# Moving one filler piece in an attention loop from step (5,4) to step (6,2), and splitting the output weights by column halves

## The chip, the cores and the metric

The kernel runs on one core of one Trainium2 chip. The metric is device time in microseconds (us) of one execution. A core has five engines that run side by side, each with its own queue: TensorE (PE in the profile, with its weight loads as PEld), VectorE (DVE), ScalarE (ACT), GpSimd (POOL) and SyncE (SP), which here only issues DMAs. Matmuls write into PSUM, which has eight banks of 128 x 512 fp32 values.

## The reference

One decoder block over 1024 tokens of width 1024, fp32. Eight attention heads of width 64 with a forget gate stand beside eight groups of a gated spatial mix; both go through one output projection; then comes a gated feed-forward part with a causal convolution of width 3.

```python
xn = rmsnorm(h, norm_mix_g);  proj = xn @ w_in
c = cumsum(log_sigmoid(proj[..., G_END:] + b_forget))
p = softmax(q k^T / 8 + c_q - c_k, causal);  att = p v
sg = u * (tril(w_s) @ rmsnorm(vg, v_gain) + b_s)        # u, vg = gelu(...)
h = h + concat(att, sg) @ w_out
h = h + (silu(conv(g)) * conv(a)) @ w_down              # a, g = rmsnorm(h) @ w_up
out = rmsnorm(h, norm_final_g)
```

The rows 512 to 1023 of `w_out` belong to `sg` and are called the gated half of the projection here; the rows 0 to 511 belong to `att`.

## The kernel before

Every fp32 operand of a matmul is split into a high part (a rounded copy, on ACT or POOL) and a low part (the difference, on DVE or POOL), and a product is three matmuls: high by high, high by low, low by high. A 128 x 1024 weight is loaded by one DMA into a tile with the tag `raw` (four buffers), and the two parts of its halves are made from there.

The attention part is a list of 40 steps (h, s): eight heads, h = 0 to 7, of five steps, s = 0 to 4. In each step TensorE's order is written out by hand (`seq` chains each matmul behind the last one). Per step:

- the transposes of the probabilities for the next step (`turn_p`, L1025): two groups of four 128 x 128 blocks, each group in a PSUM bank with the tag `b`; in s = 3 and s = 4 the groups are cut differently, but it is always one bank for a group. ACT makes the high part (L1026), then DVE the low part (L1027), and then the bank is free again;
- the products with V for this step's two groups (`values`, L1041), whose sums stand in further `b` banks until ACT (L1049) and DVE (L1050) have taken them;
- the logits of the next head (L977, L978), into two tiles of two banks; DVE adds the mask and takes the row minimum (L990), ACT takes the exponential (L1000). The last head has no next one, so its steps have no logits;
- where the table `FILLS` has the step, a filler piece.

There are four `b` banks in all: for the transposes, for the sums of the products with V, for the transposed row sums (L939), and for the filler pieces.

The filler is the gated half of the output projection, `sg_out`: 16 pieces (two column halves of eight token tiles). A piece is 12 matmuls of 512 columns (L1065 to L1067), an addition of the input rows on DVE (L1069), a store of the sum to memory (`hpd`, L1070, SP), and, ahead of them, a load of the input rows into a `raw` buffer (L1061, SP). Three pieces stand before the loop, and 13 at (0,0), (0,2), (0,4) and at (h,2) and (h,4) for h = 1 to 5; the last one at (5,4). A piece reads the gated half's weights, four tiles `whl` of 128 x 2 x 512, and the transposed gate outputs `sgT`, four tiles with the tag `G`.

These two sets of buffers are used again. The attention half's weights (`wo_load`, called in program order at (7,0)) go, for the row blocks k = 0 and 1, into the four `whl` tiles, and for k = 2 and 3 into two `G` tiles; the attention outputs of the heads 4 and 5 (`pair_half(2)`, L951 to L953, POOL) and of the heads 6 and 7 (`pair_half(3)`, L955 to L957, DVE and ACT) go into the other two `G` tiles. So all of these wait for the last filler piece. The weights' splits are on POOL: a cast (L1096) and a subtraction (L1097) for each of the two column halves of each k.

After the loop comes the attention half of the output projection, `wmm` (L1271 to L1273): for the first four token tiles the blocks k = 0, 1, 2 for the column half 0 of all four tiles, then the same for the column half 1, then k = 3 for both. DVE adds `hpd` (`hadd`, L1281), ACT and DVE normalise (L1288 to L1291), and TensorE transposes (`flip`, L1309) between the products of the later token tiles. The up projection's first weights (`upw_a`, L1220; `upw_b`, L1239) are loaded into `raw` buffers that the attention weights free; their splits are on ACT (L160) and DVE (L166), their sums on POOL (L1243 to L1251). `row_tail` sends a head's row sums through memory to a broadcast tile (ACT's DMA L941, SP's DMA L942), which `pair_half` multiplies with.

TensorE's order is by hand, while the order on DVE, ACT, POOL and SP inside the loop is set by a planner that takes, at each point of its own model of time, the earliest instruction in program order that is ready; so an instruction can stand in its queue ahead of one that comes earlier in the code. Each queue runs in order: a DMA on SP that waits holds back those behind it.

Of the kernel before, what the change touches and what calls it, by code (L numbers as in the profile page):

```python
# [12 lines left out]
ALU = mybir.AluOpType  # L13
# [6 lines left out]
WARM = 8  # L20

FILLS = {(-1, j): 1 for j in (6, 4, 2)} | {(h, s): 1 for h in range(6) for s in ((0, 2, 4) if h == 0 else (2, 4))}
FCFG = ("b", 4, 4)


# [38 lines left out]
def after(tc, later, earlier):  # L64
    tc.add_manual_dep(later.ins, earlier.ins.name, mybir.DependencyInfo(
        mybir.DependencyClass.NoSync, mybir.DependencyReason.DATA), reason="order")
# [3 lines left out]
def block_kernel(ctx: ExitStack, tc: tile.TileContext, xT, xtok, wuv, wv0, wva, wvk, wvl, wqk, cpk, bfv,  # L70
                 ggain, g2r, gfr, wsp, woa, wos, wup, wdn, out):
    nc = tc.nc
    act, dve, pool, pe, sp = Line(nc.scalar, tc), Line(nc.vector, tc), Line(nc.gpsimd, tc), nc.tensor, nc.sync
# [6 lines left out]
    drm = ctx.enter_context(tc.tile_pool(name="drm", bufs=1, space=bass.MemoryType.DRAM))  # L80
    FILL = FILLS
    FTAG, FB, BB = FCFG
    psa = tc.alloc_tile_pool(name="psa", bufs=4, space=bass.MemoryType.PSUM)
# [12 lines left out]
    def sb(tag, shape, dt=F32):  # L96
        return (raws if tag == "raw" else late if tag in LATE else early).tile(shape, dt, tag=tag, bufs=BUFS[tag], name=nm(tag))
# [10 lines left out]
    def f32(ap):  # L108
        return ap.bitcast(F32)
# [75 lines left out]
    def xs(n, hl, k):  # L185
        return XS[n][k // 2][:, hl, k % 2, :]
# [7 lines left out]
    def xr(n, k):  # L194
        return RAW[n][k // 2][:, k % 2, :]
# [8 lines left out]
    def ring(dt=F32R, n=512):  # L204
        rn[0] += 1
        return sb(RTAG[(rn[0] - 1) % 6], [P, 2, n], dt)
# [76 lines left out]
    w = ring()  # L283
    split_w(ua[0][:, 0, :], (w[:, 0], w[:, 1]), "dve")
    for o in (slice(0, 256), slice(256, 512)):
        h, l, src = xs("B11", 0, 0)[:, o], xs("B11", 1, 0)[:, o], xr("x11", 0)[:, o]
# [483 lines left out]
    def sg_load(hf, floor=None):  # L770

        wrs = []
        for kp in range(2):
            wr = sb("raw", [P, 2, 512])
            queued[:] = [sp.dma_start(out=wr, in_=wos[hf, kp])]
            after(tc, queued[0], floor or loads[0])
            wrs += [wr[:, 0, :], wr[:, 1, :]]
        return wrs
# [88 lines left out]
    def head_loads(h):  # L867
        ab = sb("x1", [P, 2, 1024], F32R)
        abs_[h] = ab
        hh = h % 2  # L870
        sp.dma_start(out=f32(ab[:, 0, :]), in_=qd[h].rearrange("s d t -> (s d) t"))
        for s in range(2):
            sp.dma_start(out=f32(ab[s * 64:s * 64 + 64, 1, :]), in_=kd[h, 0])
        sp.dma_start(out=f32(a2s[0:64, hh, :]), in_=qd[h, 0])
        if h == 1:
            sp.dma_start(out=f32(a2s[64:67, hh, :]), in_=ncd[0:3, 0, :])
        loads[h] = sp.dma_start(out=f32(b2s[0:64, hh, :]), in_=kd[h, 1])
        if h:
            loads[h] = sp.dma_start(out=f32(b2s[64:67, hh, :]), in_=ncd[1:4, 1 + h, :])
        rows[h] = sml.tile([P, 8], F32, tag="rs", name=nm("rs"))  # L880

    whs, wrs = [], sg_load(0, floors["sp"])
# [62 lines left out]
    def pair_half(p, o):  # L945

        if attT[p] is None:
            attT[p] = sb("A" if p < 2 else "G", [P, 2, 1024], F32R)
        f, t = attF[p], attT[p]
        if p < 3:  # L950
            pool.tensor_tensor(out=f[:, 0, o], in0=f[:, 0, o], in1=f[:, 1, o], op=ALU.mult)  # L951
            pool.tensor_copy(t[:, 0, o], f[:, 0, o])
            pool.tensor_tensor(out=t[:, 1, o], in0=f[:, 0, o], in1=f32(t[:, 0, o]), op=ALU.subtract)  # L953
        else:
            dve.tensor_tensor(out=f[:, 0, o], in0=f[:, 0, o], in1=f[:, 1, o], op=ALU.mult)  # L955
            act.copy(t[:, 0, o], f[:, 0, o])
            dve.tensor_tensor(out=t[:, 1, o], in0=f[:, 0, o], in1=f32(t[:, 0, o]), op=ALU.subtract)  # L957
# [5 lines left out]
    def place():  # L963
        return psa.tile([P, 1024], F32, tag="L", bufs=2, name=nm("pl"))
# [53 lines left out]
    def turn_p(g):  # L1018

        ptr = bank()  # L1020
        pt = sb("pt", [P, 2, 512], F32R)
        for half, k, j0, c, w in spans(g):
            for j in range(j0, 4 * half + 4):
                o = c + (j - j0) * P
                seq(pe.transpose(ptr[:, o:o + P], places[g[0], j // 2][j % 2][:, k * P:(k + 1) * P], ident))  # L1025
        casts.append(act.copy(pt[:, 0, :], ptr))  # L1026
        los.append(dve.tensor_tensor(out=pt[:, 1, :], in0=ptr, in1=f32(pt[:, 0, :]), op=ALU.subtract))  # L1027
        return pt
# [3 lines left out]
    def values(g, pt):  # L1032
        h, x = g[0], None
        for half, k, j, c, w in spans(g):
            new = (half, k) in ((1, 0), (0, 2))
            if new:
                po[half] = bank()
            o = (j - 4 * half) * P
            for s in range(2):
                lhs = V[k // 2][:, k % 2, h, :, :].rearrange("p s d -> p (s d)")  # L1040
                seq(pe.matmul(po[half][:, o:o + w], lhs, pt[:, s, c:c + w], start=(new and s == 0),  # L1041
                              stop=(s == 1 and (half, k) in ((1, 6), (0, 3))), skip_group_check=True))
            if (half, k) in ((1, 6), (0, 3)):
                p, hh = h // 2, h % 2
                q = slice(half * 512, half * 512 + 512)
                r = slice(hh * 64, hh * 64 + 64)
                if attF[p] is None:
                    attF[p] = sb("H", [P, 2, 1024])
                x = act.copy(attF[p][r, 0, q], po[half][64:128, :])  # L1049
                dve.tensor_tensor(out=attF[p][r, 0, q], in0=po[half][0:64, :], in1=attF[p][r, 0, q], op=ALU.add)  # L1050
        return x
# [30 lines left out]

    wo = []

    def wo_load(ks):
        for k in ks:
            wr = sb("raw", [P, 1024])
            after(tc, sp.dma_start(out=wr, in_=woa[k]), loads[6])
            if k < 2:
                w = [sb("whl", [P, 2, 512], F32R) for _ in range(2)]  # L1090
            else:
                t = sb("G", [P, 2, 1024], F32R)
                w = [t[:, :, hf * 512:hf * 512 + 512] for hf in range(2)]
            for hf in range(2):
                src = wr[:, hf * 512:hf * 512 + 512]
                pool.tensor_copy(w[hf][:, 0], src)  # L1096
                pool.tensor_tensor(out=w[hf][:, 1], in0=src, in1=f32(w[hf][:, 0]), op=ALU.subtract)  # L1097
            wo.append(w)

    STEPS = [[(h, g) for g in GROUPS[n:n + 2]] for h in range(8) for n in range(0, 9, 2)]  # L1100

# [34 lines left out]
    for n, step in enumerate(STEPS):  # L1136
        h, s = n // 5, n % 5
        if s == 0 and h < 6:
            head_loads(h + 2)
        if h == 7 and s == 0:  # L1140
            for _ in filler:
                pass
            wo_load((0, 1))
            wo_load((2, 3))
        if h in (2, 4, 6) and s == 4:
            for o in (slice(0, 512), slice(512, 1024)):
                pair_half(h // 2 - 1, o)
        now, turned = turned, [turn_p(g) for g in STEPS[n + 1]] if n + 1 < len(STEPS) else []
        last, due = due, []
        if n == 34:  # L1150

            held, last = last, []
        if n == 35:
            held, last = last, held
        if n == 36:
            last = held
        if s == 1 and h % 2 == 0:
            attF[h // 2] = sb("H", [P, 2, 1024])
        if s == (1 if h < 7 else 2):
            recips[h] = dve.reciprocal(rows[h], rows[h])  # L1160
        out_copy = None
        for c, (g, pt, js) in enumerate(zip(step, now, NEXT[s])):
            out_copy = values(g, pt) or out_copy
            last_copy = out_copy
            if h < 7:
                for j in js:
                    due.append((h + 1, j, logits_min(h + 1, j, logits_mm(h + 1, j, place()))))
            if s == (1 if h < 7 else 2) and c == (h == 7):
                row_tail(h)

        for e in last:
            x = logits_exp(*e)
            after(tc, x, out_copy or casts[-1])
        fill((h, s))
        if n == 2:
            vh = sb("A", [P, 2, 4, 256])
            sp.dma_start(out=vh, in_=vu.rearrange("h p m c -> p h m c"))
        if n in UPPER:
            tt = UPPER.index(n)
            low = evac_v(tt, 1, vh[:, tt // 4, tt % 4, :])  # L1180
            after(tc, low(), los[-1])
            after(tc, vhigh[0], exs[-1])
# [155 lines left out]
    prev = None  # L1338
    for tt in (0, 4, 1, 5, 2, 3, 6, 7):
# [12 lines left out]
        prev = tt  # L1352
# [458 lines left out]
```

## Time and profile before

| | |
|---|---|
| median of 3 runs | 1050.65 us (1050.4 to 1051.11) |
| the profiled execution | 1051.8 us, of which the span is 1050.1 us |
| TensorE busy | 1038.9 us, 99% of the span |
| VectorE, ScalarE, GpSimd busy | 891.3, 563.4, 218.8 us |
| granted clock of TensorE | 0.998 of full speed |

The span has these stretches around the change: attention with its fillers from about 214 us to 363.2 us, of which 322.0 to 340.3 is head 5, 340.4 to 353.3 head 6 and 353.3 to 363.2 head 7; the attention half of the output projection from 363.2 to 412.6; the up projection after it. Times inside the span are counted from its start. A matmul of 512 columns is shown with a duration of 0.39 us, but the next one starts 0.23 us after it, so distances between starts are read, not durations.

### The profile page before, as it was taken

The numbers are of one execution on the slowest core, as the hardware profiler recorded it, in microseconds if no ns is written. First come the engines' busy times: TensorE is split into PE (matmuls) and PEld (weight loads), VectorE is DVE, ScalarE is ACT, GpSimd is POOL, SyncE is SP. The second block draws the span as 40 slices with busy tenths as digits, with TensorE's granted clock in tenths as the row PEclk, the third lists the DMA queues.
The fourth block names the chain that finished last, engine by engine and source line by source line (L and its number), as shares of the span: only waits on it lengthen the run. The fifth ranks groups of instructions, "written<-read, shape, count | busy, mean of one in ns | idle before, by whom it ended". The sixth has DMA issues, their size and how long they took to land.

```text
span 1050.1 us, 14270 instructions
## 1 busy us (share of the span) xinstructions
PE 1038.9 (99%) x4998; PEld 870.7 (83%) x4998; DVE 891.3 (85%) x1302; ACT 563.4 (54%) x1003; POOL 218.8 (21%) x165
## 2 busy tenths in 40 slices
PE   8999999999999999999999999999999999999997
PEld 6988888988888888888888888888888888888886
DVE  6898887888887779998999989899897866897774
ACT  6777533457776746644444444444444554454654
POOL 0000241400421640344333423323331000000000
PEclk9999999999999999999999999999999999999999
DMA  9622558785655544222255332332322998333442
GB/s 335 217 96 81 160 151 250 221 257 177 192 153 161 171 153 149 80 97 84 85 179 168 122 117 74 131 120 70 128 83 81 304 346 299 104 99 98 143 120 100
DMA packets 67451, 161.66 MB, mean 154 GB/s; under 512 B 8094, under 2 KB 9238, under 8 KB 67380
## 3 DMA queue, kind: packets, MB, share of 16 engines
q1 hardware_dynamic: 67108, 160.72, 47.5%
q8 instruction: 39, 0.64, 0.3%
q14 instruction: 32, 0.26, 0.1%
q10 hardware_dynamic: 272, 0.04, 0.0%
HBM read 115.68 MB, written 45.05 MB: 153 GB/s over the span
## 4 chain that ended last, share of the span: by engine, by line
PE 91%; DVE 3%; DMA 3%; ACT 2%; issue 1%; SPq 0%; POOL 0%; ACTq 0%; POOLq 0%; DVEq 0%
PE k L1624 20%; PE qc L1364 11%; PE qa L1364 11%; PE qd L1364 11%; PE qb L1364 5%; PE pb L270 5%; PE ps L270 5%; PE pb L1041 2%; PE pb L1025 2%; PE qc L510 2%; PE qd L510 2%; PE qa L510 2%; PE pl L977 1%; PE pl L978 1%; PE pf L1065 1%; PE pf L1067 1%
## 5 line engine op out<-in xcount | busy, mean ns | idle before, releaser
L1624 PE MATMUL k<-whb,wha 128*128 128x512 f32 (+1 forms) x936 | 209.8, 386 | 0.0
L1624 PEld LDWEIGHTS k<-whb,wha 128*128 128x128 f32 x936 | 174.1, 188 | 35.8 <-DVE wha L166 0.2
L1364 PE MATMUL qc<-xT,whb 128*128 128x512 f32 x540 | 129.9, 389 | 0.2 <-ACT whb L160 0.2
L1364 PE MATMUL qa<-xB,wha 128*128 128x512 f32 x528 | 127.4, 390 | 0.0
L1364 PEld LDWEIGHTS qc<-xT,whb 128*128 128x128 f32 x540 | 101.3, 188 | 21.6 <-ACT whb L160 0.5
L1364 PEld LDWEIGHTS qa<-xB,wha 128*128 128x128 f32 x528 | 98.8, 188 | 20.8 <-DVE wha L166 0.4
L160 ACT CAST wha<-sg 128x512 fp32r<-128x512 f32 x77 | 47.7, 622 | 96.6 <-PE k L1624 83.8
L160 ACT CAST whb<-sg 128x512 fp32r<-128x512 f32 x82 | 50.6, 618 | 87.6 <-PE qc L1364 67.4
L166 DVE TENSOR_TENSOR wha<-sg,wha 128x512 fp32r<-128x512 f32 x77 | 52.7, 687 | 39.3 <-ACT wha L160 39.0
L1364 PE MATMUL qd<-xB,whb 128*128 128x512 f32 x264 | 63.7, 389 | 0.0
L1364 PE MATMUL qd<-xT,whb 128*128 128x512 f32 x264 | 63.7, 389 | 0.0
L1364 PE MATMUL qb<-xT,whb 128*128 128x512 f32 x252 | 61.0, 389 | 0.0
L1026 ACT CAST pt<-pb 128x512 fp32r<-128x512 f32 x72 | 40.4, 585 | 38.2 <-PE pb L1025 33.1
L166 DVE TENSOR_TENSOR whb<-sg,whb 128x512 fp32r<-128x512 f32 x82 | 57.0, 697 | 4.4 <-ACT whb L160 4.3
L1248 POOL TENSOR_TENSOR sg<-raw 128x512 f32<-128x512 f32 x20 | 31.2, 1562 | 140.0 <-DVE whb L166 79.9
L1364 PEld LDWEIGHTS qd<-xT,whb 128*128 128x128 f32 x264 | 49.5, 188 | 10.5 <-DVE u L1471 0.3
L1364 PEld LDWEIGHTS qd<-xB,whb 128*128 128x128 f32 x264 | 49.6, 188 | 10.3
L1027 DVE TENSOR_TENSOR pt<-pb,pt 128x512 fp32r<-128x512 f32 x72 | 47.2, 686 | 11.6 <-ACT pt L1026 11.1
L1364 PEld LDWEIGHTS qb<-xT,whb 128*128 128x128 f32 x252 | 47.2, 188 | 10.0 <-DVE whb L166 0.3
L1041 PE MATMUL pb<-pt,V 128*128 128x512 f32 (+3 forms) x192 | 49.6, 362 | 0.4 <-DVE pt L1027 0.3
L1251 POOL TENSOR_TENSOR sg<-sg,raw 128x512 f32<-128x512 f32 x20 | 33.3, 1665 | 63.5 <-DVE whb L166 63.5
L1249 POOL TENSOR_TENSOR sg<-sg,raw 128x512 f32<-128x512 f32 x20 | 35.2, 1758 | 47.2 <-issue 44.6
(422 smaller groups left out, 2243.4 us busy)
## 6 DMA issues: line engine op xcount, KB each, us to landing
raw<-wup SPq DMA_DIRECT2D x44, 512.0 KB
sg<-hx SPq DMA_DIRECT2D x77, 256.0 KB
hx<-hs SPq DMA_DIRECT2D x44, 256.0 KB
hx<-ca SPq DMA_DIRECT2D x35, 256.0 KB
xT<-wdn SPq DMA_DIRECT2D x28, 256.0 KB
x<-kd SPq DMA_DIRECT2D x24, 256.0 KB
A<-xtok SPq DMA_DIRECT2D x8, 512.0 KB
raw<-wqk SPq DMA_DIRECT2D x8, 512.0 KB
```

Source lines behind the costliest of these rows:

```text
L160: act.copy(h, src)
L166: return eng.tensor_tensor(out=l, in0=src, in1=f32(h), op=ALU.subtract)
L270: pe.matmul(banks[m], xs(n, xi, k)[:, ms], w[:, wi, :], start=(first and k == 0 and c == 0 and (own or m % 2 == 0)), stop=(k == 3 and c == ...
L510: pe.matmul(ps, w[:, wi, ks], xs(n, xi, k), start=(first and c == 0), stop=(c == 11), skip_group_check=True)
L1026: casts.append(act.copy(pt[:, 0, :], ptr))
L1027: los.append(dve.tensor_tensor(out=pt[:, 1, :], in0=ptr, in1=f32(pt[:, 0, :]), op=ALU.subtract))
L1041: seq(pe.matmul(po[half][:, o:o + w], lhs, pt[:, s, c:c + w], start=(new and s == 0), stop=(s == 1 and (half, k) in ((1, 6), (0, 3))), ski ...
L1248: pool.tensor_tensor(out=s[0], in0=a21, in1=a22, op=ALU.add)
L1249: pool.tensor_tensor(out=s[1], in0=s[0], in1=a11, op=ALU.add)
L1251: pool.tensor_tensor(out=s[3], in0=s[1], in1=a12, op=ALU.add)
L1364: pe.matmul(ps, w[:, wi, ks], xb[:, xi, k, :], start=(first and n == 0), stop=(n == 11), skip_group_check=True)
L1624: pe.matmul((banks[bk + m] if ps is None else ps)[:, o], xh[:, xi, ms], wh[:, wi, o], start=((first and p_ == 0 or new) and n == 0), stop= ...
```

## The change

Two edits. The 16th filler piece is issued at step (6,2) instead of at (5,4). And the splits of the attention weights, which went k by k (both column halves of k = 0, then of k = 1, and so on), go by column halves: half 0 of k = 0, 1, 2; half 1 of k = 0, 1, 2; then both halves of k = 3. They are chained, each cast behind the subtraction before it. The four loads come in the same order as before, now all ahead of the first split in program order.

```diff
 FILLS = {(-1, j): 1 for j in (6, 4, 2)} | {(h, s): 1 for h in range(6) for s in ((0, 2, 4) if h == 0 else (2, 4))}
+FILLS[6, 2] = FILLS.pop((5, 4))
...
-    def wo_load(ks):
-        for k in ks:
+    def wo_load():
+        wrs = []
+        for k in range(4):
             wr = sb("raw", [P, 1024])
             after(tc, sp.dma_start(out=wr, in_=woa[k]), loads[6])
             if k < 2:
...
                 t = sb("G", [P, 2, 1024], F32R)
                 w = [t[:, :, hf * 512:hf * 512 + 512] for hf in range(2)]
-            for hf in range(2):
-                src = wr[:, hf * 512:hf * 512 + 512]
-                pool.tensor_copy(w[hf][:, 0], src)
-                pool.tensor_tensor(out=w[hf][:, 1], in0=src, in1=f32(w[hf][:, 0]), op=ALU.subtract)
+            wrs.append(wr)
             wo.append(w)
+        prev = None
+        for k, hf in [(k, hf) for hf in range(2) for k in range(3)] + [(3, 0), (3, 1)]:
+            w, src = wo[k][hf], wrs[k][:, hf * 512:hf * 512 + 512]
+            c = pool.tensor_copy(w[:, 0], src)
+            if prev is not None:
+                after(tc, c, prev)
+            prev = pool.tensor_tensor(out=w[:, 1], in0=src, in1=f32(w[:, 0]), op=ALU.subtract)
...
         if h == 7 and s == 0:
             for _ in filler:
                 pass
-            wo_load((0, 1))
-            wo_load((2, 3))
+            wo_load()
```

## The prediction

> **What bounds the kernel now.** I read the busy table, the chain of waits, TensorE's waits by releaser, and then the timelines of the engines from 334 to 386 us, where the moved piece, its old and new place and everything that waits for its buffers lie.
>
> ```profile
> PE 1038.9 (99%) x4998; PEld 870.7 (83%) x4998; DVE 891.3 (85%) x1302; ACT 563.4 (54%) x1003; POOL 218.8 (21%) x165
> PE 91%; DVE 3%; DMA 3%; ACT 2%; issue 1%; SPq 0%; POOL 0%; ACTq 0%; POOLq 0%; DVEq 0%
> PE pb L1025 <- DVE pt L1027: 0.9, 1, 0.9
> 340.30:353.30 13.00, 13.00 (x86) 11.64 (x84) 11.97 (x25) 9.59 (x22) 13.00 (x15) 1.00 0.40 135
> 353.30:363.20 9.90, 8.65 (x56) 6.83 (x55) 7.56 (x16) 7.44 (x18) 4.65 (x5) 1.00 0.52 152
> 363.20:412.60 49.40, 49.39 (x243) 40.82 (x242) 38.63 (x59) 26.17 (x52) 11.26 (x8) 1.00 0.48 175
> ```
>
> TensorE sets the time. Moving a piece changes none of its work, so the change is worth only what it adds to or takes from TensorE's gaps. In the stretches around the piece the waits view names a wait of 0.9 us on DVE's low part, and the window rows (length, then busy time of PE, PEld, DVE, ACT, POOL, clock, DMA) put the open time into head 7: 9.90 - 8.65 = 1.25 us. The output projection behind it has none. The clock is 1.00 everywhere.
>
> The gap that matters stands where head 6 ends, and beside it stands the same place one head earlier, which has the piece:
>
> ```profile
> 334.34 0.27 PE L1025 MATMUL pb<-ident,gg 128*128 128x128 f32 x1
> 336.12 1.06 PE L1025 MATMUL pb<-ident,t 128*128 128x128 f32 x8
> 337.54 0.45 PE L1065 MATMUL pf<-whl,G 128*128 128x512 f32 x1
> 340.36 1.03 PE L1025 MATMUL pb<-ident,t 128*128 128x128 f32 x8
> 343.92 1.04 PE L1025 MATMUL pb<-ident,t 128*128 128x128 f32 x8
> 347.18 0.41 PE L1025 MATMUL pb<-ident,t 128*128 128x128 f32 x2
> 349.94 0.27 PE L1025 MATMUL pb<-ident,gg 128*128 128x128 f32 x1
> 351.91 1.08 PE L1025 MATMUL pb<-ident,H 128*128 128x128 f32 x8
> 353.34 0.62 PE L1025 MATMUL pb<-ident,H 128*128 128x128 f32 x4
> 354.86 0.66 PE L1025 MATMUL pb<-ident,H 128*128 128x128 f32 x4 [0.90 <-DVE pt L1027]
> 355.46 1.20 PE L1041 MATMUL pb<-pt,V 128*128 128x512 f32 x4
> ```
>
> These rows are the step starts: (5,3) at 334.34, (5,4) at 336.12, the piece at 337.54, (6,0) at 340.36, (6,1) 343.92, (6,2) 347.18, (6,3) 349.94, (6,4) 351.91, (7,0) 353.34. At (7,0) TensorE turns one group of four blocks and stops: the second group needs a `b` bank, and all four are held, two by the transposes of 351.91, one by the sums of head 6, one by the group just turned. The bank comes when the low part of the 351.91 group is done. At (6,0) the same eight transposes run without a stop, since the piece stands ahead of them. The Trainium skill (Perfetto Trace Analysis, Optimization Strategy) says that the same gap in a saturated engine, coming back, can mean too few PSUM tiles to give out. The trace agrees so far as it has one such place; by that rule a second place without a piece gets a second gap, as the sum below has it from rows.
>
> **Part one: the piece leaves (5,4).** TensorE reaches (6,0) at 337.54 instead of 340.36: 2.82 us early. The bank there comes from these:
>
> ```profile
> 336.91 0.60 ACT L1000 ACTIVATE wy<-wy,mn 128x384 f32<-128x384 f32 x1
> 337.63 1.07 ACT L1026 CAST pt<-pb 128x512 fp32r<-128x512 f32 x2
> 338.25 1.29 DVE L1027 TENSOR_TENSOR pt<-pb,pt 128x512 fp32r<-128x512 f32 x2 [0.34 <-ACT pt L1026]
> 341.94 1.29 DVE L1027 TENSOR_TENSOR pt<-pb,pt 128x512 fp32r<-128x512 f32 x2 [0.70 <-ACT pt L1026]
> 343.15 1.33 DVE L990 CUSTOM_DVE_ANT_0 H<-pl,t,lim 128x1024 f32<-128x1024 f32 x1
> 353.50 1.07 ACT L1026 CAST pt<-pb 128x512 fp32r<-128x512 f32 x2
> 354.12 1.29 DVE L1027 TENSOR_TENSOR pt<-pb,pt 128x512 fp32r<-128x512 f32 x2 [0.45 <-ACT pt L1026]
> ```
>
> The low part of the first group starts at 338.25 and takes half of 1.29 and a little, so the bank is there at about 339.0; TensorE stands from 337.94 (four transposes take 0.4) to 339.0: 1.06 us. The next bank, for the sums of head 6, comes with the second low part at 339.55, so the products start at 339.6: with 0.82 us of transposes a step starting at 337.54 wanted them at 338.36, a loss of 1.25 us. The gap at (7,0) confirms the size: there 355.46 - 353.34 - 0.82 = 1.30 us.
>
> Then (6,0) to (6,2) follow, 3.56, 3.26 and 2.76 us long by the starts above. DVE could be the next to stop TensorE: after its 0.70 us of idle time at 341.94 it works nearly without a break, with the row minima (L990) from 343.15. Moved up, it can start the first one at about 342.25 (two low parts after its reciprocal), is done at 343.55, and TensorE wants that place at 337.54 + 1.25 + 3.56 + 0.8 + 0.46 = 343.6: no stop, and no slack either. I take 0 and keep 0.6 as the upper end, from a row where DVE came 1.5 us late in the same step of head 2:
>
> ```profile
> 271.82 0.50 PE L977 MATMUL pl<-x 128*128 128x512 f32 x1 [0.63 <-DVE mn L990]
> ```
>
> So the end of (6,2) is at 337.54 + 1.25 + 9.58 = 348.4, against 349.94.
>
> **Part two: the piece at (6,2).** 12 matmuls, 340.36 - 337.54 = 2.8 us less 0.1: 2.74. It fits the banks as it does at (5,2). Step (6,3) then starts at 351.1 instead of 349.94: +1.2. From there head 6 now looks like head 5 after its piece at (5,2): from the start of (5,3) to the bank it is 339.0 - 334.34 = 4.66 us, against 354.86 - 349.94 = 4.92 in head 6 now, where ACT was still behind with exponentials. So the second group of (7,0) starts at 351.1 + 4.66 = 355.8 against 354.86: +0.9. The gap at (7,0) thus stays, and one like it comes at (6,0). Head 7 behind it is a chain of transposes, ACT and DVE that I shift as it is. Sum for attention: +1.25 at (6,0), -0.26 at (7,0): **+1.0 us**.
>
> The piece's other instructions: its addition on DVE (0.69 us) goes from the first step of head 6 into (6,3), as (5,2)'s does; its load on SP was early and stays; its store on SP moves from 341.27 to about 352.5 (351.1 and DVE's turn), where it can stand ahead of the fourth weight load (L1088, 347.15 before) and the up projection's first, which wait for later things anyway (part three, with the rows).
>
> **Part three: what waits for the piece.** POOL's and SP's rows:
>
> ```profile
> 338.58 0.62 POOL L952 CAST G<-H 128x512 fp32r<-128x512 f32 x1 [0.21 <-PE pf L1067]
> 347.07 1.17 POOL L1096 CAST whl<-raw 128x512 fp32r<-128x512 f32 x2
> 355.42 2.53 POOL L1097 TENSOR_TENSOR G<-raw,G 128x512 fp32r<-128x512 f32 x2
> 363.21 0.45 PE L1271 MATMUL pb<-whl,A 128*128 128x512 f32 x1
> 371.44 0.39 PE L1271 MATMUL ps<-whl,A 128*128 128x512 f32 x1
> 379.60 0.39 PE L1271 MATMUL pb<-G,G 128*128 128x512 f32 x1
> 341.27 0.33 SPq L1070 DMA_DIRECT2D hpd<-raw  x1
> 347.15 0.33 SPq L1088 DMA_DIRECT2D raw<-woa  x1
> 354.37 3.94 SPq L1239 DMA_DIRECT2D raw<-wup  x2
> 363.19 0.45 SPq L942 DMA_DIRECT2D H<-rsd  x1
> 367.27 1.29 DVE L955 TENSOR_TENSOR H<-H 128x512 f32<-128x512 f32 x2 [2.55 <-DMA H<-rsd]
> 369.86 4.68 DVE L166 TENSOR_TENSOR wha<-raw,wha 128x512 fp32r<-128x512 f32 x4
> L166 DVE TENSOR_TENSOR wha<-raw,wha x4: 685/1228/1777, 369.9 to 372.8; 128x512 fp32r<-128x512 f32 x4
> 370.62 1.67 POOL L1243 TENSOR_TENSOR raw<-raw,raw 128x512 f32<-128x512 f32 x1 [12.67 <-DVE wha L166]
> 380.48 0.69 DVE L1281 TENSOR_TENSOR pt<-pb,pt 128x512 f32<-128x512 f32 x1 [5.94 <-PE pb L1273]
> ```
>
> POOL's cast waited for the piece's first three matmuls: 1.04 us behind its start. With the piece at 348.4 - 0.05 that is 349.4. Six half-splits took 347.07 to 357.95 (355.42 + 2.53), 1.81 each. What is left of pair_half(2) is two casts at 1.17 / 2 and two subtractions and a product at 2.53 / 2, 4.9. So half 0 of k = 0, 1, 2 is done by 349.4 + 4.9 + 3 x 1.81 = 359.7, half 1 by 365.1, k = 3 by 368.7. TensorE wants them from 363.21, 371.44 and 379.60, each plus 1.0: slacks of 4.5, 7.3 and 11.9. In the old order k = 2 half 0 would be the fifth split, 363.3, against 364.64 + 1.0 (the first G row of the products): also in time, so the new order buys nothing here, and costs nothing while these slacks hold.
>
> It does hold the `raw` buffers longer: k = 0's is free after the fourth split, 361.5, the last one at 368.7, and the up projection's four loads, now from behind 347.15 to 358.0 (354.37 + 3.94 less the 0.33 of an issue), wait for them. If SP's order stays, head 7's row sums (L942, at 363.19) stand behind them and go at 369.1; the DVE products that need them come 4.08 us after (363.19 to 367.27), 373.2, done with the ACT casts and subtractions 2.6 later at 375.8, and wanted at 380.6. Behind them the four L166 take 4.68: 380.5, and the first addition L1281 is due at 381.5. It fits with 1.0 us to spare. I take 0 for this part.
>
> **Sum.** +1.0 us on the profiled execution's 1051.8 (span 1050.1 and 1.7 around it). That execution is 1.15 above the median shown, so on the median it is 1050.65 + 1.0 = 1051.7. 0.2% of it is 2.1 us, about what a measurement of this kernel can tell from no change.
>
> **Rivals.** *Slower: the freed buffers come too late.* Place: SP's queue and DVE before the first L1281. It decides once the last up-projection load goes more than 1.0 us after 368.7. For it: POOL's subtractions are 1.29 beside DVE work that reads PSUM, but L1243 took 1.67 beside L166. If the eight subtractions of the splits ran at 1.67, that is 8 x 0.4 = 3.2 us more, of which 2.2 reach TensorE: +3.2, 1053.9. The fourth weight load may also wait for the buffer of k = 0, freed at 361.5, and the splits of k = 3 behind it. Against it: the planner may put the row sums ahead of the loads. The Trainium skill (SBUF - State Buffer, Who interferes with whom) has a rule that speaks for this rival: a DVE instruction with two inputs in SBUF contends with a GpSimd instruction that reads SBUF. The trace agrees: the four L166 took 685 to 1777 ns here while L1243 ran. By rows, as a mechanism here: splits until 368.7 beside L955 to L957 from 367.3, at most two such pairs at +1.1 each, 2.2 us, inside L1281's slack of 5.9 if SP is not late, and +1.2 beyond it if it is.
>
> *No change: the gap only moves.* If the planner puts ACT's casts of (6,0) ahead of the exponentials, the bank comes up to 0.6 us sooner, and with ACT and DVE ahead the gap at (7,0) is halved: +0.65 - 0.7, 1050.6. For it: the casts at 337.63 stand behind exponentials. Against it: (5,3) to (5,4) show the same order with everything on time.
>
> *Faster: head 7 closes up.* With a piece's time of rest, ACT and DVE enter head 7 early. The gaps there are 1.30 at (7,0) and about 1.5 more up to 363.21 (9.87 us for some 7.0 of issue); if nothing opened at (6,0), the most is -2.8: 1047.9. Against it: at (7,0) the bank, not a late engine, is short, and nothing but a piece at (6,4) would cover that.
>
> **How the numbers follow.** My case 0.44 (own range +0.4 to +1.9, 1051.0 to 1052.6), no change 0.16, slower 0.32, faster 0.08. Within 0.2% are the first two, 0.60. The range goes from 1049.3 (half of the most in head 7) to 1055.0 (1053.9 and the contention); it leaves out the lower half of the faster case and the tail of the slower one, where several of its costs add up.
>
> **What would show it.** In the new profile: a wait of transposes on L1027's low part of about 1 us at 338, and one still at the start of head 7; (6,3) at about 351.1; the first L1271 at 364.1 to 364.3; POOL's last L1097 ending near 369; no gap of TensorE from there to 413. I am wrong if (6,0) runs without a stop, if L1271 to L1273 or the first L1309 wait for POOL, DVE or a DMA, or if the output projection's stretch is longer than 49.4 us.

## The result and the profile after

The changed kernel takes 1055.82 us (median of six runs, 1053.39 to 1056.7) against 1050.53 for the kernel before (six runs); the ratio is 1.0044 with a 95% interval of 1.0034 to 1.0054, that is 3.6 to 5.7 us slower. The profiled execution is one of 1056.7 us, with a span of 1055.0. All ratios here and below are taken over the fast executions, so they are not exactly the ratios of the medians, and one execution of 3725 us of the run called piece_only below is left out of its ratio.

The first view is the chain of waits and TensorE's waits by releaser, for the changed kernel. Line numbers behind the edits are higher by one to five than before: L1026 to L1028 are the transposes, ACT's cast and DVE's low part, L943 is the load of a head's row sums, L956 to L958 are pair_half(3), L167 the split of the up projection's weights, L1296 the last step of the norm (`xn`), L1314 the transposes of `xn`. They shift again with the edits of each experiment, so in the rows of other runs go by the names of the tiles.

```profile
PE 84%; DVE 5%; DMA 3%; ACT 2%; POOL 2%; issue 1%; SPq 1%; DVEq 0%; ACTq 0%; POOLq 0%
PE pb L1026 <- DVE pt L1028: 1.5, 2, 0.8
PE pb L1042 <- DVE pt L1028: 0.3, 1, 0.3
PE ps L1314 <- DVE xn L1296: 3.4, 2, 3.0
```

TensorE's share of the chain fell from 91% to 84%; DVE's rose from 3 to 5, and POOL and SP are in it now. There are two waits of transposes for a bank in attention where there was one, and a wait of 3.4 us in the output projection, which had none.

The next rows are TensorE's timeline of the changed kernel, from head 5's start to the first product of the up projection; columns as in the prediction.

```profile
320.65 1.03 PE L1026 MATMUL pb<-ident,H 128*128 128x128 f32 x8
...
336.19 0.62 PE L1026 MATMUL pb<-ident,t 128*128 128x128 f32 x4
337.64 0.66 PE L1026 MATMUL pb<-ident,t 128*128 128x128 f32 x4 [0.82 <-DVE pt L1028]
...
353.01 0.62 PE L1026 MATMUL pb<-ident,H 128*128 128x128 f32 x4
354.35 0.66 PE L1026 MATMUL pb<-ident,H 128*128 128x128 f32 x4 [0.71 <-DVE pt L1028]
...
362.69 0.45 PE L1276 MATMUL pb<-whl,A 128*128 128x512 f32 x1
...
389.26 1.09 PE L1314 MATMUL ps<-ident,xn 128*128 128x128 f32 x8 [3.05 <-DVE xn L1296]
391.47 1.12 PE L1314 MATMUL ps<-ident,xn 128*128 128x128 f32 x4 [0.32 <-DVE xn L1296]
...
417.52 0.84 PE L1369 MATMUL qa<-xB,wha 128*128 128x512 f32 x3
```

The two ends that the prediction does not show for the kernel before, head 5's start and the first product of the up projection:

```profile
322.01 1.03 PE L1025 MATMUL pb<-ident,H 128*128 128x128 f32 x8
412.66 0.84 PE L1364 MATMUL qa<-xB,wha 128*128 128x512 f32 x3
```

Two stretches tell where the time went. From the start of head 5 to the first product of the output projection it is 362.69 - 320.65 = 42.04 us, against 363.21 - 322.01 = 41.20 before: +0.84. From there to the first product of the up projection it is 417.52 - 362.69 = 54.83, against 412.66 - 363.21 = 49.45: +5.38. What comes behind takes about 637.5 us in both. That head 5 starts 1.36 us earlier here is a spread between executions: ahead of the moved piece the order of the work is the same, and over all profiles of this document head 5 starts between 319.69 and 322.40. The sum is -1.36 + 0.84 + 5.38, within 0.1 of the 4.9 us between the spans.

So nearly all of the loss is in the output projection, and it begins on SP. SP's, DVE's and POOL's timelines of the changed kernel:

```profile
352.76 0.33 SPq L1090 DMA_DIRECT2D raw<-woa  x1
359.42 2.25 SPq L1225 DMA_DIRECT2D raw<-wup  x2
363.26 4.18 SPq L1244 DMA_DIRECT2D raw<-wup  x2
367.55 1.13 SPq L1282 DMA_DIRECT2D pt<-hpd  x1
368.72 0.45 SPq L943 DMA_DIRECT2D H<-rsd  x1
377.09 1.29 DVE L956 TENSOR_TENSOR H<-H 128x512 f32<-128x512 f32 x2 [12.90 <-DMA H<-rsd]
379.68 4.68 DVE L167 TENSOR_TENSOR wha<-raw,wha 128x512 fp32r<-128x512 f32 x4
384.28 0.68 DVE L1286 TENSOR_TENSOR pt<-pb,pt 128x512 f32<-128x512 f32 x1
387.93 1.28 DVE L1296 SCALAR_TENSOR_TENSOR xn<-pt,ss,g2b 128x1024 f32<-128x1024 f32 x1
365.80 1.29 POOL L1104 TENSOR_TENSOR G<-raw,G 128x512 fp32r<-128x512 f32 x1
```

POOL's last split ends at 367.09, and the last of the four up-projection loads (`wup`) goes behind it, at 367.11 (363.26 + 4.18 less the 0.33 of an issue). Head 7's row sums (L943) stand behind that load and behind one `hpd` load, whose issue takes 1.13 us, and go at 368.72. They reach DVE not 4.1 us after that, as before, but 8.4 (377.09). From there DVE has no break: products, splits of `wha`, additions, `xn`. The first addition starts 21.6 us after the first product of the projection, against 17.3 before (380.48 - 363.21).

A second loss follows from the first. The windows of the changed kernel around that stop (length, then busy time of PE, PEld, DVE, ACT, POOL, clock, DMA share, GB/s):

```profile
386.00:389.20 3.20, 0.21 (x1) 0.00 (x0) 3.20 (x7) 2.37 (x6) 3.12 (x3) 1.00 0.90 357
389.20:391.00 1.80, 1.74 (x10) 1.18 (x10) 1.76 (x3) 1.05 (x3) 1.80 (x2) 0.80 0.99 310
391.00:393.00 2.00, 1.68 (x7) 1.43 (x7) 1.92 (x4) 1.99 (x5) 2.00 (x2) 0.50 0.70 227
393.00:395.00 2.00, 2.00 (x11) 1.63 (x10) 1.84 (x3) 0.43 (x2) 0.79 (x1) 0.83 0.59 229
395.00:397.00 2.00, 2.00 (x13) 1.64 (x13) 1.36 (x3) 0.59 (x1) 0.00 (x0) 1.00 0.33 113
```

After 3.05 us without a matmul TensorE's granted clock is 0.80, 0.50 and 0.83 for nearly 6 us: 1.80 x 0.20 + 2.00 x 0.50 + 2.00 x 0.17 = 1.7 us of full-speed time. The waits of 3.4 and this make 5.1 of the 5.38. The drop of the clock is not in every execution: three of the six show a mean clock of 0.997 and take 1055.78 to 1056.7 us, the other three show 0.999 to 1.000 and take 1053.39 to 1055.87.

### The profile page after: what moved, and what is told of

It is laid out like the page before. It is cut to its first block, busy times and chain, and to the rows that moved or that the text cites. A ratio compares the mean times of both kernels' runs of the same rounds, so it can differ in the third digit from the quotient of the medians.

```text
span 1055.0 us, 14271 instructions
## 1 busy us (share of the span) xinstructions
PE 1040.5 (99%) x4998; PEld 870.2 (82%) x4998; DVE 891.0 (84%) x1302; ACT 562.8 (53%) x1003; POOL 220.4 (21%) x165
## 4 chain that ended last, share of the span: by engine, by line
PE 84%; DVE 5%; DMA 3%; ACT 2%; POOL 2%; issue 1%; SPq 1%; DVEq 0%; ACTq 0%; POOLq 0%
PE k L1629 20%; PE qc L1369 11%; PE qd L1369 11%; PE qa L1369 10%; PE qb L1369 5%; PE ps L271 5%; PE pb L271 4%; PE pb L1042 2%; PE pb L1026 2%; PE qc L511 2%; PE pl L978 2%; PE qd L511 2%; PE qa L511 2%; PE pl L979 2%; PE pf L1066 1%
## 5 line engine op out<-in xcount | busy, mean ns | idle before, releaser
L1369 PEld LDWEIGHTS qc<-xT,whb 128*128 128x128 f32 x540 | 101.3, 188 | 21.6 <-ACT whb L161 0.5
L167 DVE TENSOR_TENSOR wha<-sg,wha 128x512 fp32r<-128x512 f32 x77 | 53.0, 690 | 38.8 <-ACT wha L161 38.6
L167 DVE TENSOR_TENSOR whb<-sg,whb 128x512 fp32r<-128x512 f32 x82 | 57.1, 698 | 4.4 <-ACT whb L161 4.3
L1028 DVE TENSOR_TENSOR pt<-pb,pt 128x512 fp32r<-128x512 f32 x72 | 47.3, 687 | 11.4 <-ACT pt L1027 11.2
```

The costliest lines, as they stand in the source:

```text
L167: return eng.tensor_tensor(out=l, in0=src, in1=f32(h), op=ALU.subtract)
L1369: pe.matmul(ps, w[:, wi, ks], xb[:, xi, k, :], start=(first and n == 0), stop=(n == 11), skip_group_check=True)
```

## The experiments

**Theory A**: the row sums of head 7 come late, since four loads that wait for POOL stand ahead of them on SP and then share the DMA engines with them; DVE is late from there on, and TensorE stops for `xn`. **Rivals**: B, POOL's later splits hold the projection themselves; C, the gap inside attention is the loss; D, the column order, which keeps the buffers of k = 0 and 1 longer, is the cause.

The medians below stand beside the kernel before on the same chip: 1050.36 for the first four runs, 1050.37 for the next four, 1050.16 for the last two. The stretches are read off each profile at the same places as above.

| run | median, us | ratio (95%) | head 5 to first product | output projection | row sums' products start after the first product |
|---|---|---|---|---|---|
| before | 1050.53 | | 41.20 | 49.45 | 4.06 |
| changed | 1055.82 | 1.0044 (1.0034 to 1.0054) | 42.04 | 54.83 | 14.40 |
| rowsum_first | 1051.05 | 1.0007 (0.9998 to 1.0017) | 42.01 | 49.45 | 3.77 |
| rowsum_act | 1051.26 | 1.0007 (0.9998 to 1.0016) | 42.03 | 49.44 | 6.75 |
| piece_only | 1053.89 | 1.0031 (1.0020 to 1.0042) | 42.02 | 52.64 | 13.20 |
| halves_only | 1050.09 | 0.9996 (0.9987 to 1.0005) | 41.19 | 49.43 | 5.73 |
| late_2 | 1051.44 | 1.0010 (1.0001 to 1.0018) | 41.19 | 50.05 | 9.38 |
| late_5 | 1058.78 | 1.0077 (1.0064 to 1.0089) | 41.20 | 56.89 | 17.51 |
| keep_54 | 1050.29 | 1.0001 (0.9992 to 1.0009) | 41.00 | 49.48 | 4.00 |
| both_ends | 1050.07 | 0.9994 (0.9985 to 1.0004) | 40.07 | 50.08 | 3.22 |
| both_ends_act | 1049.44 | 0.9995 (0.9986 to 1.0004) | 40.09 | 49.89 | 3.70 |
| before_rowsum | 1050.10 | 1.0000 (0.9991 to 1.0009) | 41.18 | 49.47 | 4.07 |

**rowsum_first: the row sums ahead of the four loads.**

```diff
-        sp.dma_start(out=attF[p][hh * 64:hh * 64 + 64, 1, :],
+        tails[h] = sp.dma_start(out=attF[p][hh * 64:hh * 64 + 64, 1, :],
...
         d = sp.dma_start(out=wr, in_=wup[i, :, 2:4, :])
         if i < AHEAD:
-            after(tc, d, loads[7])
+            after(tc, d, tails[7])
...
-        sp.dma_start(out=wr, in_=wup[i, :, 0:2, :])
+        d = sp.dma_start(out=wr, in_=wup[i, :, 0:2, :])
+        if i < AHEAD:
+            after(tc, d, tails[7])
```

> The changed kernel, with the up projection's first four weight loads ordered behind the load of head 7's row sums on SP. Theory A (the row sums come late because four loads that wait for POOL stand ahead of them on SP, and then share the DMA engines): the row sums' load is issued near 363 us instead of 368.7, their DVE products (L956 there) start at about 367 to 369 instead of 377.1, TensorE does not wait for xn before the first transposes of the normed tokens, its clock stays at 1.00, and only attention's +0.8 us is left: about 1051.4 us, 4.4 below the changed kernel. Rival B (POOL's later splits themselves hold the output projection): the wait for xn stays, 1055 to 1056. Rival C (the gap inside attention is the loss): 1055 as well.

Its SP, DVE and POOL timelines:

```profile
363.45 0.45 SPq L943 DMA_DIRECT2D H<-rsd  x1
363.99 1.01 SPq L1225 DMA_DIRECT2D raw<-wup  x2
368.83 0.33 SPq L1244 DMA_DIRECT2D raw<-wup  x1
368.18 1.77 DVE L956 TENSOR_TENSOR H<-H 128x512 f32<-128x512 f32 x2 [2.26 <-DMA H<-rsd]
367.51 1.29 POOL L1104 TENSOR_TENSOR G<-raw,G 128x512 fp32r<-128x512 f32 x1
```

The projection is 49.45 us again, to the hundredth, while POOL's splits end as late as in the changed kernel (367.51 + 1.29 = 368.80 with the first product at 364.41, so 4.39 after it; 4.40 in the changed kernel). That rules out B. Attention keeps its 0.8 us, and the whole is 0.7 above the kernel before: that is what is left of C, and it is at the edge of what the runs resolve.

**rowsum_act: the row sums on another queue.**

```diff
-        sp.dma_start(out=attF[p][hh * 64:hh * 64 + 64, 1, :],
+        (act if h == 7 else sp).dma_start(out=attF[p][hh * 64:hh * 64 + 64, 1, :],
```

> The changed kernel, with the load of head 7's row sums issued by ScalarE's queue instead of SP's; the four weight loads stay where they are. It separates the place in SP's queue from the sharing of the DMA engines. If the queue's order is all: the load goes at about 363, its products start at 367 to 368, no wait for xn, 1051.4. If the sharing of the DMA engines with the weight loads is most of it: the products start at 372 or later, and some of the 3 us wait stays, 1053 to 1055.

```profile
362.80 4.19 SPq L1244 DMA_DIRECT2D raw<-wup  x2
362.89 0.51 ACTq L943 DMA_DIRECT2D H<-rsd  x1
368.98 1.29 DVE L956 TENSOR_TENSOR H<-H 128x512 f32<-128x512 f32 x2 [4.24 <-DMA H<-rsd]
```

Here the four loads are where the changed kernel has them, and the row sums are issued beside them instead of behind them. From issue to DVE it takes 6.1 us instead of 8.4, still 2.0 more than the 4.1 before; that this comes of sharing the DMA engines with the loads on SP is likely, but not shown apart. The products, though, start at 6.75 after the first product, 7.65 earlier than in the changed kernel, and nothing waits. The queue's order is the larger part, and enough.

**piece_only and halves_only: one edit at a time.** The first is the kernel before with only `FILLS[6, 2] = FILLS.pop((5, 4))`, the second the changed kernel without that line.

> The kernel before, with only the filler piece moved to (6,2); splits k by k as before. Theory A: the same place on SP, the last of the four loads still waits for the eighth split (about 367), so the row sums go at 368 to 369 and the wait for xn is there again: 1054.5 to 1056.5. The column order does nothing for the first product either way: k = 2's half 0 is split by 361.5, wanted at 363.8. Rival D (the column order holds the buffers of k = 0 and 1 longer and so is the cause): about 1051.4.

> The kernel before, with only the splits' column order. Theory A: the splits begin with the piece at 337.5, the last ends near 358 as before, so the row sums go at about 363 and nothing waits: 1050.5, within 0.7 of the kernel before. Rival D: 1053 or more.

The moved piece alone makes most of the loss (1.0031, with the same stop for `xn`; 1053.89 us is below the 1054.5 to 1056.5 expected), the column order alone none (0.9996), which answers D as a cause by itself. It is not free under the moved piece, though: the row sums' products come 1.2 us later with it (14.40 against 13.20). The chained splits follow each other at 1.92 us (351.68 to 353.59 for the first two casts), where the kernel before took 1.81. TensorE's stops for `xn` in piece_only are 3.1 us together, the longest 2.5, and in the profiled execution the clock stayed at 1.00 behind them:

```profile
PE ps L1310 <- DVE xn L1292: 3.1, 2, 2.5
385.00:400.00 15.00, 11.95 (x64) 9.90 (x65) 14.24 (x23) 9.85 (x21) 6.87 (x4) 1.00 0.68 233
```

Between these two profiles the projection differs by 2.2 us (54.83 and 52.64), of which 1.7 is the clock that the longer stop lost and the shorter one kept. Two other executions of piece_only show a mean clock of 0.997 and take 1055.35 and 1055.41 us, so the shorter stop may lose it too in some executions; no trace of them was kept.

**late_2 and late_5: the suspected cost by itself,** in the kernel before, with n = 2 and 5:

```diff
+        if h == 7:
+            for j in range(n):
+                sp.dma_start(out=pass_[j], in_=rsd[h].rearrange("a b -> (a b)").unsqueeze(0).to_broadcast((P, 1024)))
         sp.dma_start(out=attF[p][hh * 64:hh * 64 + 64, 1, :],
```

> The kernel before, with two extra copies of 512 KB each (head 7's row sums, repeated, into a scratch tensor in memory) on SP right ahead of the load of head 7's row sums; nothing else moves. Theory A says that the lateness of that load alone makes the loss, and that it is free up to a deadline: its DVE products (L955 there) may start up to about 373.2 us (first addition due at 380.5, less 4.7 for the four wha splits, less 2.6 for the products themselves). Two copies at some 300 GB/s are 3.5 us: products at about 371, inside the deadline, no wait for xn, 1050.4. If lateness costs from the first microsecond on: 1053 to 1054.

> The same with five copies, 8.7 us: products at about 376, 2.8 past the deadline. Theory A: TensorE waits 2.5 to 3 us for xn at the first transposes of the normed tokens, and its clock drops after that for some microseconds in some runs (up to 1.7 us more): 1053 to 1055. If the moved piece and not the lateness is the cause: 1050.4.

Both make the products later than I said: counted from the first product of the projection, 9.38 us against 7.8 expected (371 - 363.2), and 17.51 against 12.8. Both also cost more: 1051.44 and 1058.78 us. In late_2, DVE's and TensorE's rows show why:

```profile
371.01 1.29 DVE L959 TENSOR_TENSOR H<-H 128x512 f32<-128x512 f32 x2 [7.88 <-DMA H<-rsd]
382.92 1.50 DVE L1295 SCALAR_TENSOR_TENSOR xn<-pt,ss,g2b 128x1024 f32<-128x1024 f32 x1
384.53 2.10 DVE L1295 SCALAR_TENSOR_TENSOR xn<-pt,ss,g2b 128x1024 f32<-128x1024 f32 x1
383.30 2.24 POOL L1249 TENSOR_TENSOR raw<-raw 128x512 f32<-128x512 f32 x1
386.69 0.66 PE L1313 MATMUL ps<-ident,xn 128*128 128x128 f32 x4 [0.65 <-DVE xn L1295]
```

The products were inside the deadline, but POOL's sums wait for the `wha` splits and moved with them, and now ran beside `xn`: 1.50 and 2.10 us instead of 1.27 and 1.28, and POOL's own 2.24 instead of 1.29. So the deadline has a soft edge, some 0.6 us of cost ahead of it. In late_5 the products of k = 3 themselves wait, which theory A as I put it did not have:

```profile
380.49 0.59 PE L1275 MATMUL pb<-G,G 128*128 128x512 f32 x1 [3.04 <-ACT G L960]
390.56 1.09 PE L1313 MATMUL ps<-ident,xn 128*128 128x128 f32 x8 [1.84 <-DVE xn L1295]
392.77 0.66 PE L1313 MATMUL ps<-ident,xn 128*128 128x128 f32 x4 [0.65 <-DVE xn L1295]
```

The clock dropped behind that first stop too:

```profile
380.00:383.00 3.00, 2.51 (x6) 1.82 (x7) 3.00 (x5) 2.43 (x5) 1.25 (x1) 0.61 0.38 152
383.00:386.00 3.00, 3.00 (x12) 2.45 (x11) 3.00 (x3) 0.00 (x0) 2.92 (x3) 0.82 0.00 0
```

That is 3.00 x 0.39 + 3.00 x 0.18 = 1.7 us again. So with the piece in its old place, a late load of the row sums gives 7.44 us in the projection (the copies that make it late also keep the DMA engines busy). Put together, the table's last two columns rise together: products up to 6.75 us after the first product cost nothing (the two runs with a piece at (6,4) lose time in another way, below), 9.38 costs 0.60, 13.20 costs 3.19, 14.40 costs 5.38 and 17.51 costs 7.44 (1.7 of each of these two is clock).

**keep_54 and both_ends: the gap inside attention.** Both have rowsum_first's order. keep_54 has `FILLS[6, 2] = FILLS.pop((5, 2))`, both_ends `FILLS[6, 4] = FILLS.pop((5, 2))`; (5,4) keeps its piece.

> The first mended kernel (row sums ahead of the four loads), with the piece of (5,2) at (6,2) and the one of (5,4) left where it was in the kernel before. It is for the gap inside attention: if a step 4 without a piece costs one gap at the next head's first step, as the prediction has it, the one at (6,0) is gone and the one at (7,0) stays: 0.8 below that mended kernel, 1050.3. If the gap comes of a piece missing anywhere in head 5: the same as the mended kernel, 1051.1.

> The same with the piece of (5,2) at (6,4), so that both last steps, (5,4) and (6,4), have a piece. Theory of the gap: none at (6,0), none at (7,0), attention 1.1 to 1.3 shorter than before. POOL starts 4 us later still: k = 2's half 0 is split by 363.5, wanted at about 363.4, so up to 0.5 of that may come back: 1049.2 to 1049.9, below the kernel before. If the gap at (7,0) is not the bank: 1050.3 or more.

TensorE's rows at the start of heads 6 and 7, first for keep_54, then for both_ends:

```profile
336.78 1.04 PE L1026 MATMUL pb<-ident,t 128*128 128x128 f32 x8
...
352.32 0.63 PE L1026 MATMUL pb<-ident,H 128*128 128x128 f32 x4
353.64 0.66 PE L1026 MATMUL pb<-ident,H 128*128 128x128 f32 x4 [0.70 <-DVE pt L1028]
```

```profile
336.53 1.03 PE L1026 MATMUL pb<-ident,t 128*128 128x128 f32 x8
...
352.30 1.03 PE L1026 MATMUL pb<-ident,H 128*128 128x128 f32 x8
```

With a piece at (5,4) there is no gap at (6,0), in both runs, and with one at (6,4) none at (7,0). Attention is 1.01 and 1.94 us shorter than in rowsum_first (42.01, to 41.00 and 40.07). both_ends gives 0.63 of it back in the projection and comes out at 1050.07, above the 1049.2 to 1049.9 expected: POOL's splits end later still, and DVE's products run beside them.

```profile
364.04 2.59 DVE L956 TENSOR_TENSOR H<-H 128x512 f32<-128x512 f32 x2 [1.72 <-DMA H<-rsd]
366.56 2.80 DVE L958 TENSOR_TENSOR G<-H,G 128x512 fp32r<-128x512 f32 x2
369.28 6.19 DVE L167 TENSOR_TENSOR wha<-raw,wha 128x512 fp32r<-128x512 f32 x4
```

**both_ends_act and before_rowsum.** The first is both_ends with the two casts of k = 3 on ACT behind its table load (`act.copy` for `pool.tensor_copy`, emitted after the loop); the second the kernel before with rowsum_first's three edits.

> Pieces at (5,4) and (6,4), the row sums ahead of the four loads, and the casts of k = 3's two splits on ScalarE behind its table load instead of on GpSimd. With both gaps gone the output projection was 0.6 us longer than before, with DVE's products L956 and L958 at 2.6 and 2.8 us for two instead of 1.3 beside POOL's splits, and TensorE waiting 0.4 us for xn. 1.2 us less of POOL work should end most of that: no wait for xn, 1049.5 (49.5 us for the output projection). If POOL is not what slows DVE there: 1050.1 as without it.

> A control: the kernel before, with only the four up-projection loads ordered behind head 7's row sums. If that order gained something of its own, it would be seen here; theory A says that before, the row sums were in time, so nothing is gained: 1050.4, within 0.7 of the kernel before.

The control shows that the new order of loads gains nothing where the row sums are in time. both_ends_act has the shortest span of the profiled executions (1047.7) and gives back 0.44 instead of 0.63, with 0.2 us of wait for `xn` left; expected was that most of it would go, and under a third did, so POOL's casts are at most a part of what slows DVE there; the rest was not looked into. Its median is 0.7 below the kernel before, with an interval for the ratio that still holds 1 (0.9986 to 1.0004). Whether it is faster is left open.

## Why the prediction was wrong

The step that failed is in part three: "I take 0 for this part", on the ground that it fits "with 1.0 us to spare". The profile shows a sign that the prediction itself named for being wrong: the first transposes of `xn` wait for DVE. Point by point:

- **The gap at (6,0)** was right in place and cause: forecast as 1.25 us with a bank wait of 1.06, measured as a wait of 0.82 on L1028 and 337.64 - 336.19 = 1.45 between the two groups, which is some 1.05 more than their 0.4. keep_54 and both_ends show that it belongs to a step 4 without a piece.
- **The gap at (7,0) stays**, also right: 354.35 - 353.01 = 1.34, against 1.52 before. Attention came out at +0.84 where I had +1.0, and DVE did not stop TensorE inside head 6.
- **POOL** was right: half 0 of k = 0, 1, 2 in time, the last split 4.4 us after the first product of the projection (forecast 368.7 - 364.2 = 4.5). No product of the projection waited for a split.
- **SP's order** was right as the bad case: the row sums behind the four loads. They were issued 6.0 us after the first product, where the forecast had 369.1 - 364.2 = 4.9: the last weight load went when forecast, 4.4 after the first product, but the `hpd` load between it and the row sums, whose issue took 1.13 us, was not in the sum. That alone uses up the 1.0 us to spare.
- **What failed above all is the time from that issue to DVE.** I took 4.08 us from the row of before. There one load of 512 KB (`hpd`) was issued in the 1.6 us ahead of it; here it was two, the last weight load and that one. The three loads behind it are the same, and the first three weight loads were about done (the DMA engines' share in the window from 367 to 368 us is 0.22). It took 8.37 here and 8.47 in piece_only. From issue to product the DMA engines moved 2.1 MB here (247 GB/s over 8.37 us) and 1.1 MB before (277 over 4.08), so the longer time goes mostly with more bytes moved meanwhile, and less with a lower rate; in what order the loads' bytes are moved was not looked into. With that one term the sum is: products at 369.1 + 8.4 = 377.5, `wha` splits done at 377.5 + 2.6 + 4.7 = 384.8, the first addition due at 381.5, so 3.3 us late. Measured: waits of 3.05 and 0.32. That the two agree so well is partly luck: with the 1.1 us of the late issue as well, the first addition came 4.3 us later after the first product than before (21.6 against 17.3). The first transposes of `xn` then came 3.8 later (389.26 - 362.69 = 26.57, against 385.95 - 363.21 = 22.74), since the additions now follow each other at 0.60 us instead of 0.68.
- **The clock** was not in the sum or in the range: another 1.7 us. With +1.0, +3.3 and +1.7, in hindsight, the sum is 1056.7 on 1050.65, against the 1055.82 measured.

So the rival "the freed buffers come too late" is what happened, and its place, SP's queue and DVE before the first addition, was as written. The point from which it was to decide was not: the last up-projection load did not go more than 1.0 us later than forecast, it went on time (4.4 us after the first product, 4.5 forecast), and the loss came of what stands behind it. Its price, 1053.9, was too low, for I looked for the extra microseconds in POOL's subtractions, which stayed at 1.28 to 1.29, and not in the transfer. The contention between DVE and GpSimd that it held in reserve showed in another pair, and was small: the second `xn` (L1296) took 2.10 us beside POOL's sums at 2.25, and TensorE waited 0.32 for it. The range's end of 1055.0 left out the transfer under load and the clock.

## What to carry to other kernels

Work that frees buffers also sets when loads go, and a load that waits holds back all that stand behind it on its queue: of a step that is moved, follow each buffer it frees to the load that takes it, and read what stands behind that load. A transfer's time to landing is not a constant of the transfer: the 4.08 us of the kernel before is the shortest of the twelve profiles here, and late_5 has 13.4. And a filler should stand where a bank is short (here the last step of a head), which one can read from the same boundary with and without it.

## What was not expected of the hardware

- The same 256 KB load took 4.1 us from issue to the first reader in the kernel before, with one load of 512 KB issued in the 1.6 us ahead of it; 6.1 when ACT's queue issued it beside the loads on SP; and 8.4 behind two of 512 KB on SP.
- A stop of 3.05 us in TensorE's work was followed by a clock of 0.80, 0.50 and 0.83 for nearly 6 us in the profiled run, one of 3.04 us (late_5) by 0.61 and 0.82; two stops of 2.5 and 0.7 us (piece_only) were not. The Trainium skill (TensorE: Matmul & The Clock Gate, Part 1: The HAM clock gate) has the clock throttled after at least one idle window of about 3.4 us; the trace has the throttling. Whether these stops were shorter than that it does not settle, since the ends of matmuls are modelled: from the start of the last matmul ahead of the stop to the start of the next it is 3.45 us here (385.81 to 389.26).
- Beside GpSimd's additions and subtractions DVE's 128 x 1024 `xn` took 2.10 us instead of 1.28, and two 128 x 512 products 2.6 and 2.8 together instead of 1.29, while GpSimd's own took up to 2.25 instead of 1.29.
